# Three more constant matmuls ahead of the first row tile in a matmul-tanh-multiply kernel

## The chip, the cores and the metric

The kernel runs on one core of one Trainium2 chip. The metric is the device time of one execution in microseconds (us). "Faster" or "slower" asks for 2%.

## The reference

```python
# x: 16 x 512 x 1024, w1 and w2: 1024 x 768, all float32, random normal
y1 = np.matmul(x, w1)
y2 = np.matmul(x, w2)
return (np.tanh(y1) * y2).astype(np.float32)
```

## The kernel before

The rows of x are cut into 64 tiles of 128. The first six ("the head") go a plain way: the row tile is loaded as float32, the first four of them are transposed on TensorE against an identity (line 223), copied to SBUF as bf16, and multiplied with weights as they arrive (lines 267 and 270). The other 58 tiles go in 29 pairs through a scheme with seven block products in place of eight, in float16 (line 401); the weights for it are combined on ScalarE and VectorE (lines 313, 318, 322) while the head runs. TensorE works through one fixed order of instructions.

Before the first row tile has landed TensorE has nothing to do. So it is given matmuls of constants, whose results nobody reads: `WARM` of them, and a few more (`FILL`) between the pieces of the first two tiles.

```python
    # remarks behind # are added for this text
    WARM = 18
    # [cut]
    EARLY = ("La0", "La1", "La2", "La3")      # weight loads issued on ScalarE's queue at once
    FILL = {"m00F0": 3, "m00F1": 6}
    ORDER = {
        "pe": """
            T00 T01 m00F0 m00G0 T10 T11 m00F1 m00G1 m10F0 T20 m10G0 ...
    # [cut]
    def feed(n, bank=banks[3]):
        for _ in range(n):
            pin(nc.tensor.matmul(bank[:, :2 * P], ones.bitcast(bf16)[:, :P], ones.bitcast(bf16), start=True, stop=True))

    pin(nc.vector.memset(ones, 2.0 ** -12))
    feed(WARM, banks[7])
    make_identity(nc, ident)
    # [cut]
    def pe_transpose_f(mt, h):                # T00, T01: the two halves of row tile 0
        for k in range(KH):
            pin(nc.tensor.transpose(banks[6 + h][:, k * P:(k + 1) * P],
                                    hf[mt][:, (h * KH + k) * P:(h * KH + k + 1) * P], ident))
    # [cut]
    def load_w(t, k):
        eng = nc.scalar if f"L{'ab'[t]}{k}" in EARLY else nc.sync
        pin(eng.dma_start(w_f[t][:, k, :], wr[t][:, k, :]))
```

Of the kernel before, what the change touches and what calls it, by code (L numbers as in the profile page):

```python
# [13 lines left out]
def kernel(  # L14
# [25 lines left out]
    F = 512  # L40
    G = N - F
    HEAD = 6
    WARM = 18
    PAIRS = (MT - HEAD) // 2
    FIRST = 6
    PLANNED = 10
# [104 lines left out]
# [7 lines that stand above are left out]
# [596 lines left out]
```

## Time and profile before

| | |
|---|---|
| time, median of the first 3 runs | 315.66 us (315.56 to 315.97) |
| TensorE busy | 307.7 us, 98% of the span of 313.8 us |
| warm-up matmuls (line 153) | 18, from 1.04 to 4.94 us |
| first row tile on TensorE | 5.24 us |
| start of the long run of steady matmuls (line 401), "the steady run" below | 46.02 us |

From the page of the kernel before, the busy times by engine, and the record of TensorE's granted clock in 40 slices of the span (9 is nine tenths or more):

```profile
PE 307.7 (98%) x1895; PEld 185.3 (59%) x1895; DVE 244.9 (78%) x571; ACT 230.7 (74%) x453; POOL 4.3 (1%) x10
...
PEclk9999999999999999999999999999999999999998
```

A TensorE busy 98% of the time says where the kernel is bound as a whole. It does not say what the first 46 us are bound by. The granted clock (the share of its full clock that TensorE was given) looks full from the first slice on. But the trace holds no entry of that clock before 4.68 us, and the view counts time without an entry as full (it reads 1.00 in every us from 1 to 5); below, the spacing of the matmuls, 213 ns before and some 109 ns after, says that the clock was at half until then.

### The profile page before, as it was taken

How to read it: one execution, taken by the hardware profiler on the slowest of the kernel's cores; microseconds unless marked ns; L12 is line 12 of the kernel's file. 1: busy time of each engine (PE TensorE's matmuls, PEld its weight loads, DVE VectorE, ACT ScalarE, POOL GpSimd, SP SyncE). 2: the span in 40 equal slices, each digit the busy share in tenths (PEclk: the TensorE clock that was granted, in tenths of full speed). 3: DMA queues.
4: the chain of work that ended last, by engine and by line, in shares of the span. 5: the costliest groups of instructions: out<-in, count | busy, mean ns of one | idle time of the engine just before them, and what ended most of it. 6: DMA issues, size and time to landing. Idle time of an engine off the chain costs nothing.

```text
span 313.8 us, 5488 instructions
## 1 busy us (share of the span) xinstructions
PE 307.7 (98%) x1895; PEld 185.3 (59%) x1895; DVE 244.9 (78%) x571; ACT 230.7 (74%) x453; POOL 4.3 (1%) x10
## 2 busy tenths in 40 slices
PE   7999999999999999999999999999999999999995
PEld 5756656566556555555555555555555655555662
DVE  2688978888888778977777897777788777778653
ACT  3778889786878777778777777877777787776552
POOL 0000000000000000000000000000000000000004
PEclk9999999999999999999999999999999999999998
DMA  7999498999999989999998999999999999995222
GB/s 287 406 400 376 100 319 229 261 269 283 291 293 293 326 246 237 256 260 275 264 274 241 248 257 237 295 264 231 253 258 283 243 277 265 250 247 153 118 103 100
DMA packets 82300, 80.59 MB, mean 257 GB/s; under 512 B 63584, under 2 KB 64096, under 8 KB 82272
## 3 DMA queue, kind: packets, MB, share of 16 engines
q1 hardware_dynamic: 81552, 78.46, 90.3%
q10 hardware_dynamic: 720, 1.77, 1.5%
q8 instruction: 15, 0.25, 0.3%
q14 instruction: 13, 0.11, 0.1%
HBM read 39.85 MB, written 25.17 MB: 207 GB/s over the span
## 4 chain that ended last, share of the span: by engine, by line
PE 82%; DMA 12%; DVE 2%; ACT 1%; issue 1%; ACTq 0%; SPq 0%; DVEq 0%
PE bank L401 82%; DMA x_f<-in_x_dram 6%; DMA wf<-in_w_dram 6%; DVE o L287 1%; DVE t L318 1%; ACT b L313 0%; ACT junk L340 0%; DVE x_h L360 0%; ACTq L250 0%; ACT x_h L362 0%; DVE t L322 0%; DVE o L437 0%; DVE xTb L244 0%; DVE p L348 0%; DVE pr L350 0%
## 5 line engine op out<-in xcount | busy, mean ns | idle before, releaser
L401 PE MATMUL bank<-t,s 128*128 128x384 f16 x696 | 131.5, 326 | 0.4 <-DVE t L318 0.4
L401 PEld LDWEIGHTS <-s 128*128 128x128 f16 x928 | 90.7, 98 | 61.2 <-issue 0.8
L401 PEld LDWEIGHTS <-xT 128*128 128x128 f16 x696 | 68.0, 98 | 47.1 <-issue 1.3
L401 PE MATMUL bank<-b,xT 128*128 128x384 f16 x464 | 93.7, 326 | 0.3 <-ACT b L313 0.3
L423 DVE TENSOR_TENSOR c<-bank,u 128x384 f32<-128x384 f32 x58 | 31.9, 553 | 41.3 <-PE bank L401 39.6
L340 ACT ACTIVATE junk<-x_f 128x1024 bf16<-128x1024 f32 x58 | 60.8, 1049 | 2.6 <-DMA x_f<-in_x_dram 2.6
L431 ACT ACTIVATE th<-c,out_r 128x384 f32<-128x384 f32 x58 | 35.3, 609 | 21.2 <-DVE c L423 21.2
L401 PE MATMUL bank<-t,xT 128*128 128x384 f16 x232 | 47.0, 325 | 0.1
L401 PE MATMUL bank<-b,s 128*128 128x384 f16 x232 | 47.0, 326 | 0.0
L418 ACT ACTIVATE u<-bank 128x384 f32<-128x384 f32 x58 | 28.3, 488 | 20.0 <-PE bank L401 19.7
L360 DVE TENSOR_SCALAR x_h<-x_f,pr 128x1024 f16<-128x1024 f32 x55 | 40.9, 746 | 0.2
L431 ACT ACTIVATE th<-bank,out_r 128x384 f32<-128x384 f32 x58 | 33.3, 575 | 6.1 <-PE bank L401 6.1
L414 ACT ACTIVATE bank<-bank 128x384 f32<-128x384 f32 x58 | 27.9, 482 | 12.6 <-DVE o L437 10.0
L437 DVE SCALAR_TENSOR_TENSOR o<-bank,out_r,th 128x384 f32<-128x384 f32 x58 | 35.4, 610 | 2.0 <-PE bank L401 2.0
L423 DVE TENSOR_TENSOR c<-bank,s 128x384 f32<-128x384 f32 x58 | 32.1, 554 | 6.1 <-PE bank L401 5.0
L437 DVE SCALAR_TENSOR_TENSOR o<-c,out_r,th 128x384 f32<-128x384 f32 (+1 forms) x57 | 34.3, 606 | 0.4 <-ACT th L431 0.2
L418 ACT ACTIVATE s<-bank 128x384 f32<-128x384 f32 x58 | 27.9, 483 | 7.3 <-PE bank L401 5.1
L267 PE MATMUL bank<-wb,xTb 128*128 128x512 bf16 x96 | 25.0, 379 | 0.0
L382 DVE TENSOR_TENSOR s<-xT 128x512 f16<-128x512 f16 x58 | 24.0, 415 | 0.2 <-DMA xT<-x_h 0.2
L270 PE MATMUL bank<-wb,xTb 128*128 128x256 bf16 x96 | 14.6, 273 | 0.0
L260 ACT ACTIVATE junk<-wf 128x768 bf16<-128x768 f32 (+1 forms) x13 | 12.8, 988 | 1.4 <-DMA wf<-in_w_dram 1.2
L267 PEld LDWEIGHTS <-xTb 128*128 128x128 bf16 x96 | 9.3, 99 | 7.5 <-DVE xTb L231 0.3
(49 smaller groups left out, 143.2 us busy)
## 6 DMA issues: line engine op xcount, KB each, us to landing
x_f<-in_x_dram SPq DMA_DIRECT2D x64, 512.0 KB, 6.2
out_dram<-o SPq DMA_DIRECT2D x62, 384.0 KB, 3.8
wf<-in_w_dram SPq DMA_DIRECT2D x12, 384.0 KB, 8.2
wf<-in_w_dram ACTq DMA_DIRECT2D x4, 384.0 KB, 7.7
xT<-x_h SPq DMA_TRANSPOSE x58, 4.0
out_dram<-o SPq DMA_DIRECT2D x3, 192.0 KB, 1.9
out_dram<-o ACTq DMA_DIRECT2D x1, 192.0 KB, 1.9
```

The costliest lines, as they stand in the source:

```text
L260: pin(nc.scalar.activation(junk[:, :n * N].rearrange("p (k n) -> p k n", n=N), w_f[t][:, k:k + n, :], ACT.Abs, accum_out=asum_w[t][:, j:j ...
L267: pin(nc.tensor.matmul(bank, hx[mt][:, k, :], w_b[t][k][:, :F], start=k == 0, stop=k == KO - 1))
L270: pin(nc.tensor.matmul(bank[:, at_:at_ + G], hx[mt][:, k, :], w_b[t][k][:, F:], start=k == 0 and mt % 2 == 0, stop=k == KO - 1, skip_group ...
L340: pin(nc.scalar.activation(junk[:, :K], xs[HEAD + 2 * i + h], ACT.Abs, scale=2.0 ** -12, accum_out=pair_sum[i][:, h:h + 1]))
L360: pin(nc.vector.tensor_scalar(xh, xs.pop(mt), pair_r[i][:, h:h + 1], None, ALU.mult))
L382: pin((nc.vector if eng == "dve" else nc.gpsimd).tensor_tensor(s, st[i, a], st[i, b], op))
L401: pin(nc.tensor.matmul(bank[:, cols], st[i, a][:, k, :], wt[t][b][:, k, cols], start=start and k == 0, stop=stop and k == KH - 1, skip_gro ...
L414: pin(nc.scalar.activation(ub[u]["b"][:, :Q], ub[u]["a"][:, :Q], ACT.Copy))
L418: pin(nc.scalar.activation(c, ub[u][bank][:, :Q], ACT.Copy))
L423: pin(nc.vector.tensor_tensor(c, ub[u][bank][:, :Q], ub[u][other], ALU.add))
L431: pin(nc.scalar.activation(th, v, ACT.Tanh, scale=rs[i][:, 0, h:h + 1]))
L437: pin(nc.vector.scalar_tensor_tensor(o[:, h, q * Q + cols.start:q * Q + cols.stop], v, rs[i][:, 1, h:h + 1], tanhs[i, h, q][:, cols], ALU. ...
```

## The change

The feed covers TensorE's wait for the first row tile. In the trace of before it left 0.30 us of that wait uncovered, and three small matmuls are meant to fill it.

```diff
@@ -40,7 +40,7 @@
     F = 512
     G = N - F
     HEAD = 6
-    WARM = 18
+    WARM = 21
     PAIRS = (MT - HEAD) // 2
```

## The prediction

> **What bounds the kernel now.** I read the page first: the chain that ended last, then the busy slices. The chain of the kernel before is, by engine and by line:
>
> ```profile
> PE 82%; DMA 12%; DVE 2%; ACT 1%; issue 1%; ACTq 0%; SPq 0%; DVEq 0%
> PE bank L401 82%; DMA x_f<-in_x_dram 6%; DMA wf<-in_w_dram 6%; DVE o L287 1%; DVE t L318 1%; ACT b L313 0%; ACT junk L340 0%; DVE x_h L360 0%; ACTq L250 0%; ACT x_h L362 0%; DVE t L322 0%; DVE o L437 0%; DVE xTb L244 0%; DVE p L348 0%; DVE pr L350 0%
> ```
>
> The 82% are the steady matmuls of line 401. None of it is the warm-up of line 153 or the transposes of line 223, which are what the change touches. The same chain in order of time says when each part begins (start, length, what):
>
> ```profile
> 2.13 10.26 DMA wf<-in_w_dram
> ...
> 12.40 7.99 DMA wf<-in_w_dram
> ...
> 20.48 8.69 DMA x_f<-in_x_dram
> ...
> 44.16 1.83 DVE t L318
> ...
> 46.02 51.72 PE bank L401 x316
> ```
>
> So for its first 29 us the path to the end runs through transfers: weights, then row tiles. Then come small ScalarE and VectorE pieces and one more row tile, and only from 46.02 us on is TensorE the path. The change sits before 5.3 us. I therefore read the order of time on TensorE for the start (start, length, what, idle before and its releaser):
>
> ```profile
> 1.04 3.90 PE L153 MATMUL bank<-ones 128*128 128x256 bf16 x18 [1.04 <-DVE ones L155]
> 5.24 1.06 PE L223 MATMUL bank<-ident,x_f 128*128 128x128 f32 x8 [0.30 <-DMA x_f<-in_x_dram]
> 6.14 0.49 PE L153 MATMUL bank<-ones 128*128 128x256 bf16 x3
> 6.65 0.39 PE L267 MATMUL bank<-wb,xTb 128*128 128x512 bf16 x1
> 6.88 0.27 PE L270 MATMUL bank<-wb,xTb 128*128 128x256 bf16 x1
> 7.41 1.09 PE L223 MATMUL bank<-ident,x_f 128*128 128x128 f32 x8 [0.26 <-DMA x_f<-in_x_dram]
> ```
>
> The 18 warm-up matmuls end at 4.94 us. TensorE then idles 0.30 us for the first row tile, works on it, and idles 0.26 us for the second at 7.41. The waits of TensorE from 0 to 60 us, with total, count and longest, show all the idle time that it has:
>
> ```profile
> PE bank L153 <- DVE ones L155: 1.0, 1, 1.0
> PE bank L223 <- DMA x_f<-in_x_dram: 0.6, 2, 0.3
> PE bank L401 <- DVE t L318: 0.4, 1, 0.4
> PE bank L401 <- ACT b L313: 0.3, 1, 0.3
> ```
>
> There are two idle places after the change: the 0.26 us at 7.41, and 0.65 us in all just before 46.02, where TensorE waits for operands that VectorE and ScalarE make. Each can swallow a small delay from before it.
>
> [...]the first 17 warm-up matmuls start 3.62 us from first to 18th, 213 ns each, and the six of the later feed (8.34 to 9.16 us) lie about 110 ns apart. The record of the granted clock does not show it, for it reads 1.00 in every stretch from 1 to 5 us; so here I go by spacing.
>
> [...]the shortest warm-up matmul in the trace took 272 ns. [...]The 18th warm-up matmul, from about 4.66 to 4.94 us, took some 275 ns by these ends: so the full clock came at about 4.66 us, with the last matmul of the feed.
>
> [...]all 32 transposes of line 223 took 272 to 329 ns (median 273) here, the first at 5.24 us among them, so they were not slow after a gap of 0.30 us.
>
> [...]In the trace every microsecond from 4 to 9 us moves 397 to 429 GB/s[...].
>
> **The change part by part.** It removes nothing. It adds three weight loads and three matmuls at the head of TensorE's queue, into a bank that nobody else uses yet. I compared the instruction streams of the two programs, buffer numbers aside and waits included: those six are the only difference on TensorE, and every other engine's stream is identical. The scheduler does not plan the feed, so no order moves.
>
> *Cost at the full clock (most likely).* The 18th starts at 4.66. The three follow at about 4.77, 4.88 and 4.99 us, 0.11 us each, and the array takes the next instruction at 4.99 + 0.11 = 5.10 us. The first transposes cannot start before their row tile has landed, and begin at 5.24. The addition is 3 x 0.11 = 0.33 us of TensorE time, but lies in the idle 0.30 us (plus the overlap of the last matmul's tail): a delay of 0 to 0.05 us.
>
> *Cost at the half clock (if the clock comes later in a run).* The three start at 4.88, 5.09 and 5.30, and the transposes at 5.30 + 0.21 = 5.51 us: 0.27 us later than 5.24. VectorE's copy of that tile (5.90 us), the feed of three (6.14) and the first two real matmuls (6.65 and 6.88) move with it. The last would start at 7.15 and leave the array free at 7.15 + 0.11 = 7.26 us. The second row tile is not there before 7.41. VectorE ends its two copies at 5.90 + 1.29 + 0.27 = 7.46 and is needed again at 8.10. So even this case is absorbed at 7.41.
>
> *Gain.* TensorE busy time goes up, idle time falls by 0.3 us, and the transposes start no earlier, since a transfer releases them. A gain can come only if the three make the clock rise earlier or stay up where it otherwise would not; in the trace it was up already. Sum on the path: 0.00 us, with at most 0.05 us unabsorbed either way.
>
> **The rivals.** (a) *The clock gains.* [...]For it: the clock came with the very last of the 18, a thin margin. Against: the three times of before lie within 0.41 us, the traced run among them in kind, and lost time before 46 us must still pass the absorbing idle places. Worth at most about 1 us in runs that miss it, so perhaps -0.3 us in a median.
>
> (b) *TensorE becomes the wait.* In-order execution makes the row tile, once landed, wait behind the feed. For it: 0.33 us added into 0.30 us idle, and 0.64 us if the clock is still half. Against: the 0.26 us (0.42 us if one counts when the array is free rather than modelled ends) before 7.41. If that slack failed, TensorE from 8 to 40 us is busy without a gap, and the delay would travel through the copies of VectorE to 46 us: at most +0.3 us.
>
> (c) *Later transfers shift.* A copy that ends later frees a row tile's buffer later. For it: buffers of the first tiles are reused by later loads. Against: the first reload lands work only from 20.5 us on, behind weights that are still coming, over 10 us after the copies. Worth 0.
>
> **Range and chances.** The best estimate is the old median, 315.66, with nothing added: 315.7. What is left is spread between runs and chips: three runs span 315.56 to 315.97, and the mechanisms above add -0.3 to +0.3. I choose 315.1 to 316.3, wider than the three runs since another chip may shift both kernels. Two per cent is 6.3 us, twenty times the largest of the mechanisms: within 2% has 0.98, and I give 0.01 to each side for what I have not thought of.
>
> **What the profile after would show.** Right: 21 warm-up matmuls from 1.04 to about 5.26 us; no idle time, or under 0.05 us, before the first transposes, which start at 5.24 to 5.30; the second group still at 7.4 with a wait for its row tile ahead of it; TensorE busy 308.0 us (0.3 more) in a span of 313.8; the long run of line 401 beginning at 46.0. The half-clock case: transposes at about 5.5, the wait before 7.41 shrunk to near nothing, the rest unmoved. Rival (a): matmuls of before at half speed after 5.2 us in some run. Rival (b): everything from 7.4 on late by the same amount, still late at 46 us. The prediction is wrong if the second group of transposes starts with no wait and the start of line 401's run moves by more than 0.3 us, or if the steady part, which no instruction of the change touches, changes its length.

The forecast's sum came to 0.00 us on the path, with at most 0.05 us unabsorbed: 315.66 us of before, put as 315.7. What the trace of before shows: the feed's first constant took 396 ns, those after it at half clock 421 ns with starts 213 ns apart, and the shortest 272 ns, which is what tells the 18th from the others. That the first transposes start no earlier rests on the trace alone, which names the tile's transfer as what released them after 0.30 us of idle time. In rival (a) a miss is an execution in which the clock steps up so late that the head runs at half speed for some us; its 1 us and -0.3 us, the lower end of what the mechanisms add, are estimates.

## The result, and the profile after

Ratios here are the mean time of one kernel's fast runs over that of the other's fast runs of the same rounds, so not quite the ratio of the medians quoted.

| | before | after |
|---|---|---|
| median | 315.62 us (314.97 to 316.60, 6 runs) | 315.67 us (315.17 to 316.13, 6 runs) |
| ratio | | 0.9999, 95% interval 0.9980 to 1.0018 |

The time is the same. The trace, though, is not what the prediction drew. In order of time on TensorE, the changed kernel (start, length, what, idle time before and its releaser):

```profile
1.04 3.99 PE L153 MATMUL bank<-ones 128*128 128x256 bf16 x21 [1.04 <-DVE ones L155]
6.21 1.06 PE L223 MATMUL bank<-ident,x_f 128*128 128x128 f32 x8 [1.18 <-DMA x_f<-in_x_dram]
7.11 0.49 PE L153 MATMUL bank<-ones 128*128 128x256 bf16 x3
7.62 0.39 PE L267 MATMUL bank<-wb,xTb 128*128 128x512 bf16 x1
...
8.27 1.09 PE L223 MATMUL bank<-ident,x_f 128*128 128x128 f32 x8 [0.15 <-DMA x_f<-in_x_dram]
```

Two things differ from before, and neither looks like three matmuls more. The 21 took only 3.99 us where the 18 took 3.90: by their spacing (213 ns at half speed, some 109 ns at full speed) the clock stepped up at about 4.2 us here and at 4.66 us before (the first entries of the granted clock in the two traces begin at 4.20 and 4.68 us). And the first row tile came 0.97 us later, so that the idle time before it grew from 0.30 to 1.18 us. All of TensorE's idle time up to 60 us in the changed kernel (total, count, longest):

```profile
PE bank L223 <- DMA x_f<-in_x_dram: 1.5, 3, 1.2
PE bank L153 <- DVE ones L155: 1.0, 1, 1.0
PE bank L401 <- DVE t L318: 0.4, 1, 0.4
```

Its long run of steady matmuls, from the chain in order of time, begins 0.61 us later than before:

```profile
46.63 263.86 PE bank L401 x1612
```

So this one pair of traces has a tile 1 us later and an end 0.4 us later (span 314.2 us against 313.8). Either the change did that, or executions differ so by themselves. The change delays no load in the program's order, but "by themselves" had to be shown.

### The profile page after: what moved, and what is told of

Its sections match the earlier page's. It is cut to its first block, busy times and chain, and to the rows that moved or that the text cites. A ratio compares the mean times of both kernels' runs of the same rounds, so it can differ in the third digit from the quotient of the medians.

```text
span 314.2 us, 5489 instructions
## 1 busy us (share of the span) xinstructions
PE 307.3 (98%) x1893; PEld 185.6 (59%) x1898; DVE 244.8 (78%) x571; ACT 230.5 (73%) x453; POOL 4.3 (1%) x10
## 4 chain that ended last, share of the span: by engine, by line
PE 89%; DMA 8%; DVE 1%; issue 1%; ACT 0%; ACTq 0%; SPq 0%; DVEq 0%
PE bank L401 84%; DMA wf<-in_w_dram 8%; PE bank L267 3%; PE bank L270 2%; DVE t L318 1%; DVE s L382 1%; PE bank L238 0%; DVE o L437 0%; ACT o L283 0%; ACTq L250 0%; SPq L250 0%; ACT junk L260 0%; PE bank L300 0%; DVE o L287 0%; DVE out_r L390 0%
## 5 line engine op out<-in xcount | busy, mean ns | idle before, releaser
L267 PE MATMUL bank<-wb,xTb 128*128 128x512 bf16 x91 | 23.6, 379 | 0.1
```

What stands on the lines that cost most here:

```text
L267: pin(nc.tensor.matmul(bank, hx[mt][:, k, :], w_b[t][k][:, :F], start=k == 0, stop=k == KO - 1))
```

## The experiments

Twelve runs, on three chips, all correct. Each is the kernel before with the lines shown. The first four ask what the feed costs and gives, the next four whether the landing of the tile is the change's doing, the last four test a theory about the clock that came out of the seventh.

**Theory A**, the prediction's: the three lie in the wait for the first tile, and what differs at 5 to 6 us is when that tile lands. **Rival B**: the three delay the landing. **Rival C**: a gain of the clock cancels a loss of order.

### The changed kernel again

```diff
-    WARM = 18
+    WARM = 21
```

> The changed kernel once more (21 constants). Theory A (the three lie in the wait for the first row tile; what differed in the two traces at 5 to 6 us is when that tile landed, which the change does not touch): time within 0.2% of the kernel before; the first transposes start when the tile lands, anywhere from 5.2 to 6.3 us, with some idle time of TensorE ahead of them that a landing explains. Rival B (the three delay the landing of the first tile itself, 5.24 to 6.21 us in the two traces): the tile lands near 6.2 us again and the time is 0.3 to 0.5 us above the kernel before. Rival C (a gain of the clock cancels a loss of order): the step to full speed comes at another time than with 18, and the time stays equal.

Measured: 316.07 us median against 316.33 of before on this chip, ratio 0.9997 (0.9978 to 1.0016). TensorE in order of time:

```profile
1.04 4.55 PE L153 MATMUL bank<-ones 128*128 128x256 bf16 x21 [1.04 <-DVE ones L155]
5.43 1.04 PE L223 MATMUL bank<-ident,x_f 128*128 128x128 f32 x8
```

The feed now took 4.55 us: all 21 at half spacing. There is no idle time before the transposes. When the tile was there is read from the next weight load on the row tiles' queue. It waits for the first weight block, which is issued together with the tile; in all six traces with a gap before the transposes it was issued 0.06 to 0.07 us after they began. Here it was issued at 5.29 us; so the tile was ready for TensorE at about 5.22 us and waited 0.21 us for the feed. (The trace's own record of the transfer agrees: it ended at 5.09 us, and transposes that wait for it start 0.14 us after its end. "Lands" below means this later moment.) That is the prediction's half-clock case. The steady run began at 46.19 us. Rival B falls: with 21, the tile landed as early as with 18. Expected by theory A was also some idle time ahead of the transposes; there was none, and the feed's own end explains it.

### No feed at all

```diff
-    WARM = 18
+    WARM = 0
```

> No warm-up at all (0 constants in place of 18; results stay right). If the feed is worth anything, it is the clock: without it the first transposes start at 5.2 to 6.2 us at half speed, and full speed comes some 3.2 to 3.7 us after them, near 9 us. TensorE does about 3.5 us of work at half speed, so is up to 1.7 us late at 9 us; of this 0.4 us fits into the wait for the second tile and 0.65 us into the idle time near 46 us: theory A expects +0.3 to +1.3 us of the whole. Rival C expects a loss of 1 us or more and full speed clearly later than 9 us[...]. A feed that is worth nothing: 0.0 to +0.2 us.

(In the two traces then at hand the clock stepped up 3.2 and 3.6 us after the first matmul at 1.04 us.)

Measured: 317.23 us median, ratio 1.0028 (1.0008 to 1.0048). Inside theory A's +0.3 to +1.3 us: 0.28% of 316.3 us is 0.9 us. (The traced execution, at 317.84 us, was the slowest of the six.)

```profile
5.21 1.94 PE L223 MATMUL bank<-ident,x_f 128*128 128x128 f32 x8 [5.21 <-DMA x_f<-in_x_dram]
...
8.23 1.92 PE L223 MATMUL bank<-ident,x_f 128*128 128x128 f32 x8
9.93 1.42 PE L153 MATMUL bank<-ones 128*128 128x256 bf16 x6
```

The same eight transposes took 1.94 us in place of 1.06, and the second group was slow too. Only within the six constants from 9.93 us on does the spacing fall, at about 11.1 us. The steady run began at 48.22 us, 2.2 us later than before, with the tile landing at the same 5.21 us. So the feed's worth is the clock, as theory A says. But full speed came later than the 9 us it named: that much rival C had expected. Whether the transposes did nothing for the clock here is taken up below the table of all traces, which speaks against it.

### Forty and eighty constants

```diff
-    WARM = 18
+    WARM = 40          # second kernel: 80
```

> Forty constants: 22 more than before[...], so the array is free at about 7.1 us instead of 4.8 to 5.0, 0.9 to 1.9 us after the first row tile landed. Theory A: the wait for the first tile is gone, the wait for the second (0.4 us) too, and what is left of the delay, 0.5 to 1.5 us, goes to the end less at most 0.65 us of idle time near 46 us: +0.2 to +1.5 us. Rival B2 (the head is bound by transfers and TensorE catches up by itself, so a delay there costs nothing): 0.0 to +0.2 us.

> Eighty constants: 62 more than before, so the array is free at about 11.4 us, 5.2 to 6.2 us after the first tile. Theory A: about 4.8 to 5.8 us of delay are left after the wait for the second tile, less 0.65 us near 46 us: +3.8 to +5.8 us, and about 4.3 us[...] more than with forty constants. Rival B2 (TensorE catches up in a head bound by transfers): less than +2 us.

(At the 109 ns between starts that the trace of before shows at full speed, 22 constants more are 2.4 us and 40 are 4.4 us.)

Measured: forty, 317.57 us median, ratio 1.0047 (1.0025 to 1.0069), 1.5 us, at the upper end of theory A's range; eighty, 322.50 us, ratio 1.0185 (1.0161 to 1.0209), 5.9 us, just above its range. (The interval takes in 2%, so the verdict is "unclear"; that it is slower by some 1.9% is clear.) In the trace with forty, and then in that with eighty:

```profile
7.37 1.04 PE L223 MATMUL bank<-ident,x_f 128*128 128x128 f32 x8
...
9.09 1.04 PE L223 MATMUL bank<-ident,x_f 128*128 128x128 f32 x8
```

```profile
12.05 1.04 PE L223 MATMUL bank<-ident,x_f 128*128 128x128 f32 x8
...
13.78 1.04 PE L223 MATMUL bank<-ident,x_f 128*128 128x128 f32 x8
```

No idle time stands before any of these groups. With forty the first group is 2.13 us later than before, the second (7.41 us before) 1.68 us, the steady run (47.46 us) 1.44 us. The wait for the second tile took 0.45 us of the delay, and only 0.24 us was lost on the way to 46 us. With eighty the three stand 6.81, 6.37 and 6.15 us later. Between the two kernels the first group moves 4.68 us and the steady run 4.71: one to one. Rival B2, a head in which TensorE catches up, falls; once the waits for the tiles are used up, every us of feed goes to the start of the steady run, and by the times (4.4 us between the two by the ratios, 4.9 by the medians) to the end.

Theory A expected the idle time near 46 us to swallow up to 0.65 us. It did not: both kernels still show the waits of 0.4 us for line 318 and 0.3 us for line 313 there. The weights' work comes late along with TensorE: with eighty, the last piece of line 318 before the steady run begins at 50.31 us, and in the trace of before at 44.16 us.

### One queue, 18 and 21

```diff
-    EARLY = ("La0", "La1", "La2", "La3")
+    EARLY = ()          # and WARM = 21 in the second
```

> The kernel before (18 constants) with its first four weight loads issued on the queue of the row tiles, in turn with them, and no longer beside them on ScalarE's queue: the first row tile then has the transfer engines more to itself. Theory A: the tile lands at 3.5 to 4.9 us in place of 5.2 to 6.2, the first transposes start when the feed is over (4.8 to 5.1 us), and there is no idle time ahead of them. The end moves little, since the later tiles and the weights come no earlier: within 0.3%. If the tile lands at 5.2 us or later all the same, its landing isn't set by sharing with the weights.

> The same with 21 constants. Theory A: the three are now in nobody's shadow at the first tile: TensorE starts the transposes 0.32 us later than with 18 on one queue at full speed (up to 0.64 us at half speed); what of it reaches the second group is 0.32 us less the wait there. In the time: 0 to +0.3 us against 18 on one queue, too little to see in the times and to be read in the trace. Rival B2: nothing moves at the second group.

(Three starts at the measured 109 and 213 ns make 0.33 and 0.64 us.)

Measured: with 18, 316.19 us median, ratio 0.9995 (0.9965 to 1.0026); with 21, 316.32 us, ratio 1.0011 (0.9972 to 1.0050). First 18, then 21:

```profile
4.64 1.04 PE L223 MATMUL bank<-ident,x_f 128*128 128x128 f32 x8
...
8.33 1.09 PE L223 MATMUL bank<-ident,x_f 128*128 128x128 f32 x8 [1.80 <-DMA x_f<-in_x_dram]
```

```profile
5.49 1.58 PE L223 MATMUL bank<-ident,x_f 128*128 128x128 f32 x8
```

By the traces' records of the transfers the first tile's ended at 3.96 and 4.03 us (before: 5.10 us), and no idle time stands before the transposes. So sharing with the weights does set the landing, and when the tile is there the feed is what TensorE waits for. How much later 21 is than 18 can't be read from this pair: 0.85 us lie between the two, but with 18 the clock stepped up at about 4.4 us and with 21 at about 6.6 us, in the middle of the transposes. As an experiment on three matmuls it is inconclusive. The earlier first tile won nothing: the second one landed later with 18 (8.33 us).

### Both kernels, one more look

No edit: the kernel before and the changed one, on the chip of the last pair.

> The kernel before, unchanged, for a second trace. Theory A: the landing of the first row tile wanders between executions by some tenths of a us up to 1 us, and so does the step to full speed of TensorE (4.2 to 5.1 us in the four traces with a feed), without the change: transposes start anywhere from 5.1 to 6.3 us. Rival B (three constants more delay the landing): with 18 it lands at 5.2 us again, within 0.1 us.

> The changed kernel, unchanged, for a third trace. Theory A: the first tile lands anywhere from 5.1 to 6.3 us, and the long run of steady matmuls starts at 45.9 to 46.8 us, later where the tile landed later. Rival B: lands at 5.9 us or later.

(For the step, the first of these has 4.2 to 5.1 us in four traces; the first entries of the granted clock put it at 4.2 to 5.7 us in the five with a feed and the original loads: the table below.)

One run each, 317.28 and 315.68 us, states unknown, so only the traces are used. With 18, then with 21:

```profile
1.03 4.02 PE L153 MATMUL bank<-ones 128*128 128x256 bf16 x18 [1.03 <-DVE ones L155]
5.80 1.94 PE L223 MATMUL bank<-ident,x_f 128*128 128x128 f32 x8 [0.75 <-DMA x_f<-in_x_dram]
...
8.81 1.58 PE L223 MATMUL bank<-ident,x_f 128*128 128x128 f32 x8
```

```profile
1.04 3.84 PE L153 MATMUL bank<-ones 128*128 128x256 bf16 x21 [1.04 <-DVE ones L155]
5.18 1.06 PE L223 MATMUL bank<-ident,x_f 128*128 128x128 f32 x8 [0.30 <-DMA x_f<-in_x_dram]
```

This settles rival B: 18 constants with a tile at 5.80 us, 21 with one at 5.18. Rival C has no support either: the step of the clock differs between two executions of the one kernel before, by more than between the two kernels, and no load was found late through the change. The pair also shows something that nobody had expected of the kernel before: its transposes took 1.94 us, just as without a feed. The clock had **not** stepped up during the feed, and did so only at about 9.9 us, inside the second group. Its steady run began at 47.57 us. In the changed kernel's first trace the tile came 0.4 us later than here and the steady run still began at 46.63. So, if nothing else differed between the two, the late clock cost at least 0.9 us in this execution.

From this came **theory D**: the clock steps up at the end of a stretch of some 3.4 us that lies differently against each execution's start, provided TensorE was busy for most of it; a gap before the first tile can spoil one such stretch. If so, three constants more, which shorten the gap, make a miss rarer. **Rival E**: the feed is worth its length. (For the 3.4 us the traces show 3.413 us, and for the four fifths of the expectations below a limit between 78% and 83%: both below the table. The 0.7 us and 1.3 us there are estimates; the late execution had a gap of 0.75 us, and its steady run began 0.94 and 1.55 us later than those of the first traces with 21 and 18.)

### Fourteen and twenty-seven constants, and both kernels a third time

```diff
-    WARM = 18
+    WARM = 14          # second kernel: 27; the third is unchanged; the fourth: 21
```

> Fourteen constants, 4 fewer than before: the feed is over at 4.0 us and TensorE idles 1.2 to 2.2 us before the first tile. Theory D, formed after the trace of the kernel before in which the first transposes ran at half speed (the clock steps up at the end of a stretch of some 3.4 us whose place against the kernel's start changes with the execution, if TensorE was busy for about four fifths of it; a gap ahead of the first tile of over some 0.7 us can spoil one such stretch, which costs about 1.3 us at the end): most executions miss the early step, so nearly all of the loss without a feed comes back: +0.15 to +0.45% in the time, full speed in the trace most likely only at 8 to 11 us. Rival E (the feed is worth its length): a quarter of the loss without a feed, less than +0.1%.

> Twenty-seven constants: over between 5.5 us (early step of the clock) and 6.8 us (late). Theory D: hardly ever a gap ahead of the first tile that spoils the step, so full speed by 7.3 us at the latest in every execution; against that the first tile waits up to 0.9 us for TensorE, of which the wait for the second takes 0.4. Time -0.1 to +0.1% against the kernel before. In the trace no idle time of TensorE over 0.7 us before the first transposes.

> The kernel before against itself, for a third trace and to see what the comparison gives where nothing differs: within 0.2%. Theory D: the transposes start at 5.1 to 6.3 us; where the gap ahead of them is over 0.7 us and the clock had not stepped up before the feed's end, they run at half speed; else at full speed.

> The changed kernel, for a fourth trace and five more rounds. Theory D: a longer feed (over at 4.8 to 5.5 us) misses the step less often than with 18; the time is 0.0 to 0.2% below the kernel before in the mean, no more than this comparison can resolve. In the trace full speed by 7.3 us.

Measured, all against the same 11 runs of before (316.16 us median):

| constants | median | ratio, 95% interval |
|---|---|---|
| 14 | 316.98 us | 1.0015, 0.9995 to 1.0036 |
| 18 (before against itself) | 316.35 us | 1.0006, 0.9977 to 1.0035 |
| 21 | 316.11 us | 0.9992, 0.9969 to 1.0014 |
| 27 | 316.54 us | 1.0004, 0.9982 to 1.0025 |

With 14, the feed ended with all matmuls at half spacing, and the late step came back:

```profile
5.78 1.94 PE L223 MATMUL bank<-ident,x_f 128*128 128x128 f32 x8 [1.58 <-DMA x_f<-in_x_dram]
...
8.78 1.04 PE L223 MATMUL bank<-ident,x_f 128*128 128x128 f32 x8
```

With 18 the clock was again not up at the feed's end, but the tile came early. The expectation for such a short gap, full speed in all transposes, failed: the first of them ran at half speed.

```profile
5.31 1.45 PE L223 MATMUL bank<-ident,x_f 128*128 128x128 f32 x8 [0.26 <-DMA x_f<-in_x_dram]
...
7.44 1.04 PE L223 MATMUL bank<-ident,x_f 128*128 128x128 f32 x8
```

And with 21, also at half speed all through the feed, there was no gap at all:

```profile
1.04 4.66 PE L153 MATMUL bank<-ones 128*128 128x256 bf16 x21 [1.04 <-DVE ones L155]
5.49 1.63 PE L223 MATMUL bank<-ident,x_f 128*128 128x128 f32 x8
...
7.67 1.04 PE L223 MATMUL bank<-ident,x_f 128*128 128x128 f32 x8
```

In both of the latter, the step fell inside the first group of transposes (it took 1.45 and 1.63 us, between 1.06 and 1.94), and the second group ran at full speed; in the last the tile landed at about 5.15 us and waited 0.34 us for the feed, and the steady run began at 46.06 us, 0.04 us later than in the trace of before.

With 27 there was no gap either (transposes at 6.36, tile at about 5.81 us), full speed from about 5.9 us, and the steady run at 46.41 us.

All traces of the original load order side by side, in us. The landing is read from the weight load, less 0.07 us, and the gap is the idle time that the trace gives. The step of the clock is the start of the trace's first entry of the granted clock; where the spacing of the matmuls changes agrees with it within 0.2 us in every trace. The last two columns are TensorE's busy share, by the profile, in the 3.41 us that end at the step, and in the 3.41 us before those; why 3.41 us is said below.

| constants | tile lands | gap before it | clock steps up | steady run starts | busy before the step | busy one stretch earlier |
|---|---|---|---|---|---|---|
| 0 | 5.21 | no feed | 11.2 | 48.22 | 100% | 74% |
| 14 | 5.78 | 1.58 | 8.8 | 47.18 | 87% | 67% |
| 18, first | 5.24 | 0.30 | 4.7 | 46.02 | 100% | 7% |
| 18, second | 5.80 | 0.75 | 9.9 | 47.57 | 100% | 78% |
| 18, third | 5.31 | 0.26 | 6.1 | 45.99 | 92% | 49% |
| 21, first | 6.20 | 1.18 | 4.2 | 46.63 | 93% | 0% |
| 21, second | 5.22 | 0 | 5.4 | 46.19 | 100% | 26% |
| 21, third | 5.18 | 0.30 | 3.9 | 45.95 | 83% | 0% |
| 21, fourth | 5.15 | 0 | 6.7 | 46.06 | 100% | 66% |
| 27 | 5.81 | 0 | 5.9 | 46.41 | 100% | 43% |
| 40 | 5.03 | 0 | 5.1 | 47.46 | 100% | 18% |
| 80 | 5.34 | 0 | 5.7 | 52.17 | 100% | 37% |

What follows for theory D. In the nine traces of this table where the clock stepped up early, it did so anywhere from 3.9 to 6.7 us. The two late cases with a feed are those with a gap of 0.75 or 1.58 us that began before the clock was up; less one stretch of 3.4 us they stand at 6.5 and 5.3 us, inside the early range. A long gap after the step (21, first: 1.18 us) did no harm. That agrees with theory D at every line.

The stretch itself is in the traces too, in the entries of the granted clock. In all fourteen traces the full clock was held for 303.79, 307.20, 310.61 or 314.03 us and for no other length. These differ by 3.413 us, and are 89, 90, 91 and 92 times 3.413 us: as if the clock changed only at the ends of fixed stretches of that length. A stretch that moved along with the work doesn't fit, for the step came 2.9 us after the first matmul in one trace (21, third) and 5.7 us after it in another whose feed had no gap (21, fourth). Counted back from each step, a stretch in which TensorE was busy for 83% or more raised the clock, and one with 78% or less didn't. The late step of the kernel before (18, second) is the clearest case. Of the two stretches before it, the first holds the gap (columns: from and to, length, TensorE busy, granted clock as the view fills it in, DMA):

```profile
3.08:6.49 3.41, 2.66 (x14) 1.00 0.95 381
6.49:9.91 3.42, 3.42 (x17) 1.00 1.03 417
```

In the second of them 2.13 us went to transposes, by the spacing of the matmuls. Were these not counted, 37% would be left, less than the 66% of constants alone that didn't raise the clock (21, fourth). So on this count the transposes of line 223 do count, at least in part.

As for the times, fourteen at +0.15% lie at the edge of theory D's range, and the interval takes in rival E's less than +0.1% as well: the times don't decide, the traces speak for D.

Whether the change makes misses rarer is **open**: one of three traces with 18 missed, none of four with 21. If that third were the true share, at 1 to 2 us a miss, 21 would win about 0.1 to 0.2%. An estimate from the table's twelve landings, with the stretches placed at random and a limit between the shares that failed and those that passed, gives fewer misses: 10 to 20% of the executions with 18, and 0 to 6% with 21. The three comparisons of 21 with 18 gave -0.01, -0.03 and -0.08%, each within +-0.2%. No version was clearly faster than either kernel.

### A second source of spread, seen in passing

The third trace of the unchanged kernel began its steady run early, at 45.99 us, yet its span is 314.7 us, 1.1 more than the third of the changed one with 45.95 us. Its waits of TensorE after 46 us hold a line that the other does not have:

```profile
PE bank L401 <- DVE c L423: 1.0, 1, 1.0
```

It stands just before 105.88 us. At the same place, 104.96 us, the trace of before stops for under 0.1 us. The trace with 27 shows the whole wait too, and those of the changed kernel again, of forty and of eighty show 0.2, 0.4 and 0.7 us for that line. In the stretch from 85 to 110 us VectorE waits 1.6 us for transposing transfers of row tiles in this trace and in that with 27, and 0.2 us in that of before. What delays them in some executions was not tested.

## Why the prediction was right, and where its steps were off

1. **The time.** 315.67 us against 315.7 predicted, nothing on the path. Right, and held in three comparisons. That the two agree to 0.03 us is luck: executions of one kernel lie over 1 us apart.
2. **The program.** Only the six instructions were added, and they hurt no other engine. The half-clock case, told in the prediction, occurred twice: transposes at 5.43 and 5.49 us against 5.51 worked out, and 46.19 and 46.06 us at the steady run. The wait for the second tile was used up both times, as foretold; but the second group stood at 7.41 us in neither (7.27 and, after transposes that were partly slow, 7.67 us).
3. **The start as a fixed schedule.** This step failed. The working treated 5.24 us for the tile and 4.66 us for the clock as constants of the kernel. The tile lands from 5.03 to 6.20 us (by the traces' own records of its end, 4.88 to 6.07 us) and the clock steps up from 3.9 to 6.7 us (9.9 us in a miss), each from one execution to the next. "No idle time, or under 0.05 us" was therefore right in two of four traces of the changed kernel, the others having 0.30 and 1.18 us; the start of the transposes at 5.24 to 5.30 us occurred in none; and "the second group still at 7.4" was 8.27 us in the first.
4. **Two places that absorb.** The first does: 0.45 us at the second tile, with forty constants. The second, the 0.65 us near 46 us, hardly does: the waits there were still whole behind a delay of 6 us. That idle time depends on weights' work which comes late when TensorE does.
5. **Transfers as the path of the first 29 us.** Too simple. In the first trace the chain ran through transfers, but TensorE's own path was close behind: of the 1.68 us by which forty constants delayed the second group, 1.44 reached the steady run. So rival (b), the delay that travels through TensorE's gapless work to 46 us, describes what happens once a feed outlasts both waits. One chain names the path that ended last and not how close the second one was.
6. **Rival (a), the clock.** It was rated as at most 1 us in executions that miss. It is real, in the kernel before; the one miss seen cost about 0.9 us or more, and a start without a feed put the steady run 2.2 us back.
7. **Busy time.** 308.0 us were expected and 307.3 recorded: the trace holds 1893 matmuls to 1898 weight loads, so a few records are missing, and the sum can't show 0.3 us.
8. **Small slips,** which move nothing. The 18th constant started at 4.64 us and took 0.30 us in the trace, not 4.66 and 0.275.

## What to carry to other kernels

In this kernel a filler in front of a transfer cost nothing that could be measured while it ended before the landing plus the slack of the next wait (0.45 us), and one for one after that (4.71 us at the steady run for 4.68 us of filler); so find that edge by doubling the filler and not from one trace. Before putting a difference at the start of two traces down to an edit, look at the unchanged kernel twice: here the landing of the first tile alone moved by half a us (5.24 to 5.80 us), and the clock's step by several (4.7 to 9.9 us). In these traces the warm-up feed was worth what it added to the busy share of a stretch of 3.41 us (83% or more let the clock step up, 78% or less didn't): in the two late cases with a feed, a gap of 0.75 or 1.58 us before the real work undid it.
